# Experts' weights in a deeper ring, narrow products in full groups, and 64-place sums off TensorE

## The chip, the cores and the metric

One core of one Trainium2 chip runs the whole kernel in one launch. The metric is the device time of an execution in microseconds; the kernel before takes 1934.09 us, the median of 3 runs (1929.53 to 1937.27).

## What is computed

The reference is a two-layer backbone over 256 tokens and 256 context tokens of width 1024. Each layer mixes tokens in four branches and then channels. The change lies in the second layer's channel mixer, eight SwiGLU experts of which each token takes the best two:

```python
def _swiglu(x, wg, wu, wd):
    return (jax.nn.silu(x @ wg) * (x @ wu)) @ wd

def _moe(x, wr, br, wg, wu, wd):
    logits = (x @ wr).astype(F32)
    _, idx = lax.top_k(logits + br.astype(F32), TOP_K)
    w = jax.nn.softmax(jnp.take_along_axis(logits, idx, axis=-1), axis=-1)
    dense = jnp.sum(jax.nn.one_hot(idx, N_EXPERTS, dtype=F32) * w[..., None], axis=-2).astype(x.dtype)
    out = dense[..., 0:1] * _swiglu(x, wg[0], wu[0], wd[0])
    for e in range(1, N_EXPERTS):
        out = out + dense[..., e:e + 1] * _swiglu(x, wg[e], wu[e], wd[e])
    return out
```

x is 256 x 1024, wg and wu of an expert are 1024 x 1408, wd is 1408 x 1024, all fp32: 17.3 MB per expert.

## The kernel before

`moe` (L1210) sorts the experts on the chip by how many tokens chose them and works on the tokens that each has, gathered into places. `CAPS` gives the places by rank and `ORDER` the rank of each position, so the eight positions, e0 to e7 here, have 64, 128, 64, 128, 64, 128, 64 and 32 places; e3 (`WIDE`) has 32 more, the "thin" ones, for the rank that may overflow. The number of an expert is read from the chip's own sort at run time, so that its loads can be addressed only then.

An expert (`expert`, L1403) is 36 loads by `load_w` (L200, the DMA itself is L204): three column groups of 512, 512 and 384 columns, each with four loads of wg and four of wu (two chunks of 128 rows a load), then two halves of wd with six loads each. A load goes into a tile of the ring `raw`. All are issued by SyncE in program order, so that one load waiting for a tile holds up the ones behind it. Rings are a base, and more that `deeper` (L180) adds in a stage: raw 5 + 3 + 5 = 13 in the experts' stage, hi and lo 4 each.

For 128 places, `split_w` makes a high and a low part of each load (ScalarE copies hi, L212; VectorE subtracts lo, L213), and `mm3` (L219 to L221) multiplies in three products. With fewer places the weights are used as loaded, in fp32: `narrow` (L1388, matmul L1394) puts the chunk's places into one of the array's column groups, two groups side by side for 64 places, four for 32, so that chunk c lands in column group c modulo 2 or 4 of one PSUM tile. Each of these products shows as two records in the trace. What stands in the column groups must then be added up. `add_up` (L1397) does so: ScalarE copies the tile out of PSUM (L1399), and a matmul per 128 columns with a selection matrix (L1401) adds and turns it at once, into a PSUM tile with the hidden channels on partitions. Silu and the product of gate and up follow there, and the result `hm` goes into the down products (L1394 again, `PM<-raw,hm`). `gated` (L1478 to L1482) weighs an expert's output, and the matmul L1506 adds it into the tokens.

The order of the work on each engine is fixed when the program is built: a scheduler with priorities lays out the parts of an expert, the sums (`later`, `catch_up`) behind some products of the next group, and the gathering of the next pair's tokens (`gather_steps`, L1344) in between. PSUM has three tiles `PM`, three `PX` and one `PB`. The ring's loads are issued as far ahead as tiles come free: the first expert's begin during the layer's output projection (`out_last`, L1069). Sixteen tiles of a pool `h` are held from the first layer to the end of the program; the experts' gathered tokens (`xe`) of the 128-place experts lie in them.

Of the kernel before, what the change touches and what calls it, by code (L numbers as in the profile page):

```python
# [41 lines left out]

MORE = 5
M_TRI, M_IOTA, M_LOW, M_SEL, M_HSEL, M_ORD, M_TOP, M_CAP, M_END = 0, 128, 256, 320, 352, 416, 424, 432, 440

# [50 lines left out]
def hybrid_backbone(ctx: ExitStack, tc: tile.TileContext, A, out, dbg=None, stop=None):  # L96
# [12 lines left out]
    pool("shift", 1).tile([128, 16], F32, name="shift")  # L109
    hpool = pool("h", 16)  # L110
    spool = pool("sg", 4)
    apool = pool("ad", 2)
    col = pool("col", 4)
    pm = pool("pm", 3, space=PSUM)
    px = pool("px", 3, space=PSUM)
# [27 lines left out]
    def sg():  # L143
        return spool.tile([128, 512], F32, name="sg")
# [52 lines left out]
    def ahead_of_rest():  # L197
        return behind() if marks else tc.high_priority(offset=AHEAD)

    def load_w(src, r0, kc, c0, n, split=True, ahead=True):  # L200
        with ahead_of_rest():
            raw = wtile("raw", F32)
            r = raw[:, :kc * n].rearrange("p (k n) -> p k n", k=kc)
            nc.sync.dma_start(r, src[r0:r0 + kc * 128, c0:c0 + n].rearrange("(k p) n -> p k n", p=128))  # L204
        return split_w(raw, kc, n, ahead) if split else r
# [863 lines left out]
    def out_last(m, ax, rows, after):  # L1069

        tiles = (2, 3)
        zs = {t: [ht(F32) for _ in range(2)] for t in tiles}
        st = {t: ln_open(4) for t in tiles}
        r = load_row(S["adarows"][0, 1, 0, :], "C")
        for g in range(2):
            tok_group(A["w_out"][1], 256 * g, m, lambda t, p: add_residual(zs[t], g, p, r, ax[t], st[t]), tiles)
        w = {(g, k0): load_w(A["w_out"][1], 128 * k0, 4, 256 * g, 256) for g in (2, 3) for k0 in (0, 4)}
        for t in tiles:
            ps = pmt()
            for g in (2, 3):  # L1080
                o = ps[:, 256 * (g - 2):256 * (g - 2) + 256]
                for k in range(8):
                    wh, wl = w[g, k & 4][:2]
                    sl = slice(128 * t, 128 * t + 128)
                    mm3(o, (m[0][k][:, sl], m[1][k][:, sl]), (wh[:, k & 3, :], wl[:, k & 3, :]),
                        k == 0 and g == 2, k == 7, skip_group_check=True)
                add_residual(zs[t], g, o, r, ax[t], st[t], quick=True)
            post_ln(zs[t], st[t], rows, quick=True)
        for t in tiles:
            after(t - 2, zs[t])  # L1090
# [119 lines left out]
    def moe(R, xm):  # L1210
# [86 lines left out]

        f = [[ph(512, "f", 4) for _ in range(2)] for _ in range(2)]
        for i in range(2):
            for k in range(2):  # L1300
                with tc.issue_after(R["act"].ins):
                    nc.scalar.activation(f[i][k], xm[i][k], AF.Copy, scale=ALPHA)

        def row(src, tile_of):
# [3 lines left out]
            return r  # L1308
        sel = {THIN: mc[:, M_SEL:M_SEL + THIN], HALF: mc[:, M_HSEL:M_HSEL + HALF]}
        ad = row(S["adarows"][1, 1, 0, :], lambda: ph(512, "adr", 2))  # L1310
        ln2b = row(A["ln2_b"][1], lambda: ph(512, "l2b", 2))
        ln2g = row(A["ln2_g"][1], at)
# [31 lines left out]
        def gather_steps(out, place, weight, sizes, between=None):  # L1344
# [11 lines left out]
            def chunk(c):  # L1356
# [8 lines left out]
                if full:  # L1365
                    sh = slice(128 * full[0], 128 * full[-1] + 128)
                    sl = slice(256 + 128 * full[0], 384 + 128 * full[-1])
                    hf = sg()
                    nc.scalar.activation(hf[:, sh], ps[:, sh], AF.Identity, scale=ac[:, 4, c, 0:1], bias=ac[:, 3, c, 0:1])
                    x = ht()  # L1370
                    nc.scalar.activation(x[:, sh], hf[:, sh], AF.Copy)
                    nc.vector.tensor_tensor(x[:, sl], hf[:, sh], x[:, sh], op=OP.subtract)
                    xe.append(x)
# [22 lines left out]

        def add_up(sums, pn, n):  # L1397
            t = sg()
            nc.scalar.activation(t[:, :n], pn[:, :n], AF.Copy)  # L1399
            for i in range(n // 128):  # L1400
                nc.tensor.matmul(sums[:, i, :], t[:, 128 * i:128 * i + 128], sel[sums.shape[-1]], start=True, stop=True)  # L1401

        def expert(wge, wue, wde, q, xe, ws, dts, first=False, thin=False, last=False, small=False, side=iter(())):  # L1403

            es, el = slice(128 * q, 128 * q + 128), slice(256 + 128 * q, 384 + 128 * q)
            hT = []
# [28 lines left out]
            def gemm(src, c0, n, sums):  # L1435
                po = None if small else pmt()
                pn = (pmt() if small else pbt()) if m else None
                for k0 in range(0, 8, 2):
                    wt = load_w(src, 128 * k0, 2, c0, n, split=not small, ahead=not (first and c0 == 0))
                    for k in range(0 if small else 2):  # L1440
                        x = xe[k0 + k]
                        mm3(po[:, :n], (x[:, es], x[:, el]), (wt[0][:, k, :], wt[1][:, k, :]), k0 + k == 0, k0 + k == 7)
                    for k in range(2 if m else 0):
                        narrow(pn, k0 + k, 8, xm, (wt if small else wt[2])[:, k, :])
                    catch_up()
                if m:
                    later.append((sums, pn, n))
                go_on()
                return po
            for c0, n in ((0, 512), (512, 512), (1024, 384)):  # L1450
                j = n // 128
                both = pxt()[:, :8 * m].rearrange("p (a c m) -> p a c m", a=2, m=m) if m else None
                part = lambda a: both[:, a, :j] if m else None
                gs = sg()
# [29 lines left out]
            for hf in range(2):  # L1484
                po = pmt()
                pn = po if small else pbt() if thin else None
                for k0 in range(0, 11, 2):
                    kc = min(2, 11 - k0)
                    wt = load_w(wde, 128 * k0, kc, 512 * hf, 512, split=not small)
                    for k in range(0 if small else kc):  # L1490
                        hi, lo = hT[k0 // 4]
                        ks = slice(128 * (k0 % 4 + k), 128 * (k0 % 4 + k) + 128)
                        mm3(po, (hi[:, ks], lo[:, ks]), (wt[0][:, k, :], wt[1][:, k, :]), k0 + k == 0, k0 + k == 10)
                    for k in range(kc if m else 0):
                        narrow(pn, k0 + k, 11, hm, (wt if small else wt[2])[:, k, :])
                    catch_up()
                go_on()
# [39 lines left out]
        for e in range(NE):  # L1537
# [12 lines left out]
            if e % 2:  # L1550
                g = ahead


# [65 lines left out]
    with phase("main") as S["main"]:  # L1619
# [54 lines left out]
        pre = ctx.enter_context(phase("pre", "right"))  # L1674
        ctx.enter_context(deeper(pre, 3, 1, 1))
        S["phase"] = pre
# [16 lines left out]
    if stop == "mid1":  # L1693
        return
    with phase("moe") as S["phase"], deeper(S["phase"], 5, 0, 0):
        moe(R, xm)
# [23 lines left out]
```

## Time and profile before

| | |
|---|---|
| median of 3 runs | 1934.09 us |
| the profiled execution | 1934.3 us |
| its span | 1932.5 us |
| granted TensorE clock, mean | 0.964 |
| TensorE busy | 1811.3 us (94%) |
| VectorE, ScalarE, GpSimd busy | 1229.8, 827.1, 513.6 us |
| DMA | 337.90 MB, mean 175 GB/s |

All times below are microseconds from the span's start. The span is what the profiler's records cover; the execution's own time is 1.8 us longer. The experts' stage lies from about 1485 to 1910; after it the last sums, a normalization and the output follow. Engines: PE is TensorE's matmuls, PEld its weight loads, DVE VectorE, ACT ScalarE, POOL GpSimd, SP SyncE, with a q behind it for the DMAs it issues. A row names line, engine, operation, written and read tiles. Matmuls overlap, so several short ones hold the array for less than the sum of the times shown: a group's busy time counts the overlap once.

### The profile page before, as it was taken

What the parts mean: (1) busy time and instruction counts of PE and PEld (TensorE: products, weight loads), DVE (VectorE), ACT (ScalarE), POOL (GpSimd) and SP (SyncE); (2) the same over time, 40 slices, a digit from 0 to 9 for tenths busy, and PEclk for the clock granted to TensorE, in tenths of its full rate; (3) what the DMA queues carried; (4) which work ended last, traced back from release to release, by engine and by line L of the source; (5) the groups of instructions that cost most, each with busy time, mean ns of one, the idle gap of its engine ahead of it and who ended that gap; (6) DMA issues with size and microseconds to landing.
All of it is one profiled execution on the core that took longest, in us unless ns stands there. A gap on an engine that the chain in (4) does not pass through costs nothing. (4 is left out here: it accounts for less than half of the span.)

```text
span 1932.5 us, 29428 instructions
## 1 busy us (share of the span) xinstructions
PE 1811.3 (94%) x10954; PEld 1433.6 (74%) x10954; DVE 1229.8 (64%) x2005; ACT 827.1 (43%) x1418; POOL 513.6 (27%) x532
## 2 busy tenths in 40 slices
PE   6899989999999889999999899989997999999994
PEld 3777967788778888799789889889795584645731
DVE  5776866765555966677758955777866473534712
ACT  3444553434344553212223544755553472623610
POOL 2353625742103610022004700266231000000001
PEclk8998989999999989999999999999997999999998
DMA  8434421113313635645756542333554999569995
GB/s 307 129 91 139 120 77 55 55 61 121 99 48 121 218 109 170 197 147 190 251 186 213 161 121 61 113 99 121 175 159 154 340 372 345 183 202 393 338 366 188
DMA packets 243935, 337.90 MB, mean 175 GB/s; under 512 B 16008, under 2 KB 158864, under 8 KB 243784
## 3 DMA queue, kind: packets, MB, share of 16 engines
q1 hardware_dynamic: 235896, 318.86, 50.2%
q0 software_dynamic: 6128, 13.99, 2.3%
q10 hardware_dynamic: 1760, 3.09, 0.5%
q8 instruction: 88, 1.44, 0.3%
q14 instruction: 63, 0.52, 0.1%
HBM read 333.77 MB, written 2.12 MB: 174 GB/s over the span
## 5 line engine op out<-in xcount | busy, mean ns | idle before, releaser
L213 DVE TENSOR_TENSOR lo<-raw,hi 128x1024 fp32r<-128x1024 f32 (+1 forms) x370 | 455.1, 1240 | 168.1 <-ACT hi L212 165.4
L212 ACT ACTIVATE hi<-raw 128x1024 fp32r<-128x1024 f32 (+1 forms) x370 | 368.2, 1001 | 433.1 <-PE PM L221 166.8
L219 PE MATMUL PM<-H,hi 128*128 128x512 f32 (+1 forms) x1104 | 386.9, 353 | 7.3 <-ACT sg L1104 2.9
L220 PE MATMUL PM<-H,hi 128*128 128x512 f32 (+1 forms) x1104 | 386.0, 351 | 1.7 <-DVE H L380 1.6
L221 PE MATMUL PM<-H,lo 128*128 128x512 f32 (+1 forms) x1104 | 384.0, 351 | 0.1
L219 PEld LDWEIGHTS PM<-H,hi 128*128 128x128 f32 x1104 | 211.7, 193 | 42.3 <-issue 4.7
L220 PEld LDWEIGHTS PM<-H,hi 128*128 128x128 f32 x1104 | 211.9, 192 | 31.0 <-DVE H L380 2.4
L221 PEld LDWEIGHTS PM<-H,lo 128*128 128x128 f32 x1104 | 210.9, 192 | 29.0 <-issue 2.7
L328 DVE SCALAR_TENSOR_TENSOR ad<-raw,silu,ad 128x512 f32<-128x512 f32 x208 | 177.4, 873 | 33.7 <-issue 15.2
L219 PE MATMUL PM<-hi,H 128*128 128x256 f32 (+2 forms) x576 | 180.1, 314 | 4.3 <-ACT in L525 4.3
L220 PE MATMUL PM<-lo,H 128*128 128x256 f32 (+2 forms) x576 | 180.3, 313 | 2.4 <-DVE lo L213 2.4
L221 PE MATMUL PM<-hi,H 128*128 128x256 f32 (+2 forms) x576 | 179.2, 311 | 0.0
L1482 POOL TENSOR_TENSOR yl<-sg,yh 128x512 fp32r<-128x512 f32 x17 | 24.1, 1415 | 404.0 <-ACT yh L1481 386.7
L219 PEld LDWEIGHTS PM<-hi,H 128*128 128x128 f32 x576 | 112.6, 195 | 13.7 <-issue 5.0
L220 PEld LDWEIGHTS PM<-lo,H 128*128 128x128 f32 x576 | 112.9, 196 | 12.0 <-issue 4.1
L1020 POOL TENSOR_TENSOR B<-B,sg 128x512 f32<-128x512 f32 (+1 forms) x48 | 62.8, 1320 | 215.0 <-DVE sg L1019 198.4
L221 PEld LDWEIGHTS PM<-hi,H 128*128 128x128 f32 x576 | 112.9, 196 | 5.3 <-issue 1.4
L1394 PE MATMUL PM<-raw,xs 128*64 128x512 f32 (+3 forms) x480 | 110.7, 567 | 0.4 <-DMA raw<-in_moe_wu_dram 0.4
L805 POOL TENSOR_TENSOR C<-C,in 128x512 f32<-128x512 f32 (+1 forms) x64 | 81.3, 1295 | 76.5 <-ACT C L804 66.5
L219 PE MATMUL PM<-hi,B 128*128 128x256 f32 x352 | 98.8, 281 | 0.0
L221 PE MATMUL PM<-hi,C 128*128 128x256 f32 x352 | 98.3, 279 | 0.0
L220 PE MATMUL PM<-lo,B 128*128 128x256 f32 x352 | 98.3, 279 | 0.0
(427 smaller groups left out, 3333.3 us busy)
## 6 DMA issues: line engine op xcount, KB each, us to landing
raw<-in_w_ada_dram SPq DMA_DIRECT2D x80, 512.0 KB, 4.3
raw<-in_moe_wd_dram SPq DMA_DIRECT2D x80, 512.0 KB, 7.1
raw<-in_w_gate_dram SPq DMA_DIRECT2D x64, 512.0 KB, 3.7
raw<-in_moe_wg_dram SPq DMA_DIRECT2D x64, 512.0 KB, 5.8
raw<-in_moe_wu_dram SPq DMA_DIRECT2D x64, 512.0 KB, 7.6
raw<-in_w_in_dram SPq DMA_DIRECT2D x54, 512.0 KB, 3.6
raw<-in_ffd_wd_dram SPq DMA_DIRECT2D x28, 512.0 KB, 3.4
raw<-in_ffd_wg_dram SPq DMA_DIRECT2D x26, 512.0 KB, 3.8
```

What stands on the lines that cost most here:

```text
L212: nc.scalar.activation(h[:, :m], raw[:, :m], AF.Copy)
L213: (nc.vector if ahead else nc.gpsimd).tensor_tensor(l[:, :m], raw[:, :m], h[:, :m], op=OP.subtract)
L219: nc.tensor.matmul(o, ah, bh, start=start, stop=False, **kw)
L220: nc.tensor.matmul(o, ah, bl, start=False, stop=False, **kw)
L221: nc.tensor.matmul(o, al, bh, start=False, stop=stop, **kw)
L328: nc.vector.scalar_tensor_tensor(acc[j], part, sc, acc[j], op0=OP.mult, op1=OP.add)
L805: nc.gpsimd.tensor_tensor(E[:, xt], E[:, xt], X[:, xt], op=OP.mult)
L1020: nc.gpsimd.tensor_tensor(mixed[c][:, xt], mixed[c][:, xt], s[:, xt], op=OP.add)
L1394: nc.tensor.matmul(po[g, :w.shape[-1]], x[:, c, :], w, start=(c < k), stop=(c + k >= kk), tile_position=(0, g.start))
L1482: nc.gpsimd.tensor_tensor(yl, y, yh, op=OP.subtract)
```

## The change

Four things, all in or around the experts:

- **The ring.** `raw` has 5 + 1 + 12 = 18 tiles. Space comes from pool `h`, which is closed before the experts (`held`): `xe` gets 16 smaller tiles of its own, the two row tiles of `out_last` and the scaled residual `f` move to other tiles. For the first expert, `spare` lists the ring of each load: 6 in raw, then 8 in the tiles of hi and lo, then the 12 new tiles of raw, so that 26 loads have a tile before one is used again.
- **Full groups.** `side_by_side` collects narrow products and issues them when a set of column groups is complete: four chunks (two loads) for 32 places, two (one load) for 64.
- **64-place sums.** `add_halves` takes the place of `add_up`: ScalarE copies the upper 64 partitions out of PSUM, VectorE adds the lower 64. Silu on ScalarE and the product with up on VectorE work on 64 x 512, and a transpose per 128 columns, 11 per expert, turns the result; ScalarE copies it into `hm`.
- **A row of ln2_b** is loaded behind e6 instead of before the experts.

```diff
-        hpool = pool("h", 16)
+        held = ExitStack()
+        hpool = held.enter_context(tc.tile_pool(name="h", bufs=16))
...
-            raw = wtile("raw", F32)
+            raw = wtile(spare.pop(0) if spare else "raw", F32)
...
-        zs = {t: [ht(F32) for _ in range(2)] for t in tiles}
+        zs = {t: [ph(512, "f", 4) for _ in range(2)] for t in tiles}
...
-        f = [[ph(512, "f", 4) for _ in range(2)] for _ in range(2)]
+        f = [xm[i] for i in range(2)]
...
-                    x = ht()
-                    nc.scalar.activation(x[:, sh], hf[:, sh], AF.Copy)
+                    x = ph(256, "xe", 16, F32R)
+                    nc.scalar.activation(x[:, :128], hf[:, sh], AF.Copy)
...
+        def add_halves(pn, n):
+            t = sg()[:HALF, :n]
+            nc.scalar.activation(t, pn[HALF:, :n], AF.Copy)
+            nc.vector.tensor_tensor(t, t, pn[:HALF, :n], op=OP.add)
+            return t
+        def side_by_side(po, kk, x):
+            k = 128 // x.shape[-1]
+            got = []
+            def add(w, c):
+                got.append((c, w))
+                if len(got) == k or c == kk - 1:
+                    for c, w in got:
+                        narrow(po, c, kk, x, w)
+                    del got[:]
+                    return True
+            return add
...
-                    for k in range(2 if m else 0):
-                        narrow(pn, k0 + k, 8, xm, (wt if small else wt[2])[:, k, :])
-                    catch_up()
-                if m:
+                    if any([add((wt if small else wt[2])[:, k, :], k0 + k) for k in range(2 if m else 0)]) or not small:
+                        catch_up()
+                if m and m < HALF:
                     later.append((sums, pn, n))
...
+                if m == HALF:
+                    pg = gemm(wge, c0, n, None)
+                    h = add_halves(pg, n)
+                    nc.scalar.activation(h, h, AF.Silu)
+                    pu = gemm(wue, c0, n, None)
+                    u = add_halves(pu, n)
+                    nc.vector.tensor_tensor(h, h, u, op=OP.mult)
+                    def turned(c0=c0, j=j, h=h):
+                        pt = pxt()[:, :HALF * j].rearrange("p (c m) -> p c m", c=j)
+                        for i in range(j):
+                            nc.tensor.transpose(pt[:, i, :], h[:, 128 * i:128 * i + 128], ident[:HALF, :HALF])
+                        nc.scalar.activation(hm[:, c0 // 128:c0 // 128 + j], pt, AF.Copy)
+                    later.append(turned)
+                    continue
...
+            if e == NE - 2:
+                ln2b = row(A["ln2_b"][1], lambda: ph(8 * HALF, "xs%d" % HALF, 2))
...
-        ctx.enter_context(deeper(pre, 3, 1, 1))
+        ctx.enter_context(deeper(pre, 1, 1, 1))
...
-    with phase("moe") as S["phase"], deeper(S["phase"], 5, 0, 0):
+    held.close()
+    with phase("moe") as S["phase"], deeper(S["phase"], NRAW, 0, 0):
+        turn["raw"] = -1
+        spare.extend(["raw"] * 6 + ["hi", "lo"] * 4)
         moe(R, xm)
```

How it moves instructions, at the two places of which the prediction speaks. First TensorE in e3, from the sum of the gate's second column group into its up products, before (`xs` and `PB` are the thin places' tokens and PSUM tile, L219 to L221 the 128-place products):

```order
L1394 MATMUL PB<-raw,xs_15067 32x512 x2
L1401 MATMUL PX<-mc,sg 128x32 x4
L1394 MATMUL PB<-raw,xs_15067 32x512 x4
L220 MATMUL PM<-lo,H 128x512
L221 MATMUL PM<-hi,H 128x512
L219 MATMUL PM<-hi,H 128x512
L220 MATMUL PM<-lo,H 128x512
L221 MATMUL PM<-hi,H 128x512
L1394 MATMUL PB<-raw,xs_15067 32x512 x2
```

and with the change (L1396 is the narrow product, L1404 the selection, L1363 the gathering, L1502 a transpose, L223 to L225 the 128-place products):

```order
L1404 MATMUL PX<-mc,sg 128x32 x4
L1396 MATMUL PB<-raw,xs_15055 32x512 x8
L1363 MATMUL PX<-oh,nh 128x256
L1363 MATMUL PX<-oh,nl 128x256
L1363 MATMUL PX<-oh,nh 128x256
L1363 MATMUL PX<-oh,nl 128x256
L1502 MATMUL PX<-cst,sg 128x128 x4
```

The eight products of a column group, which came as 2, 4 and 2 with 128-place products between, stand in one run of eight. In all of e3 the narrow products stand in 21 runs of up to four (a run of eight counted as two): of the first column group's gate, four of two; then six of four at 512 columns, four of four at 384; and for the down products two of four and 4, 3, 1, 3 and 3 products.

Second TensorE in e6, from the sum of the first up product to the down products, before (`xs` and `hm` are the 64-place tokens and hidden values):

```order
L1401 MATMUL PX<-mc,sg 128x64 x4
L1394 MATMUL PM<-raw,xs_16939 64x512 x6
L1401 MATMUL PX<-mc,sg 128x64 x4
L1394 MATMUL PM<-raw,xs_16939 64x512 x4
L1394 MATMUL PM<-raw,xs_16939 64x384 x2
L1401 MATMUL PX<-mc,sg 128x64 x4
L1394 MATMUL PM<-raw,xs_16939 64x384 x8
L1401 MATMUL PX<-mc,sg 128x64 x3
L1394 MATMUL PM<-raw,xs_16939 64x384 x6
L1401 MATMUL PX<-mc,sg 128x64 x3
L1394 MATMUL PM<-raw,hm 64x512 x13
```

and with the change (L1489 is the new transpose):

```order
L1396 MATMUL PM<-raw,xs_16917 64x512 x6
L1489 MATMUL PX<-cst,sg 128x64 x4
L1396 MATMUL PM<-raw,xs_16917 64x512 x8
L1396 MATMUL PM<-raw,xs_16917 64x384 x6
L1489 MATMUL PX<-cst,sg 128x64 x4
L1396 MATMUL PM<-raw,xs_16917 64x384 x10
L1396 MATMUL PM<-raw,hm 64x512 x2
L1489 MATMUL PX<-cst,sg 128x64 x3
L1396 MATMUL PM<-raw,hm 64x512 x11
```

The sums of gate and of up, each behind some products, are gone; one run of transposes per column group is left. The last of the three stands behind two down products, where the selection before stood behind six up products of the same column group.

## Rows read from the trace of the kernel before

**Rows 1.** Windows, e0 to e7: start:end, length, engines (instructions), PEclk, DMA share, GB/s.

```profile
1485.60:1534.20 48.60, 48.60 (x217) 21.27 (x217) 9.65 (x27) 16.59 (x38) 0.00 (x0) 0.99 0.78 272
1534.20:1592.00 57.80, 57.80 (x286) 48.21 (x285) 48.60 (x57) 43.28 (x74) 3.98 (x3) 1.00 1.03 378
1592.00:1632.20 40.20, 40.20 (x194) 16.48 (x193) 7.20 (x17) 6.57 (x12) 2.55 (x2) 1.00 0.94 326
1632.20:1734.00 101.80, 101.80 (x476) 56.65 (x475) 51.87 (x61) 50.23 (x79) 4.87 (x4) 1.00 0.61 204
1734.00:1772.30 38.30, 38.30 (x184) 16.88 (x184) 6.29 (x15) 6.70 (x12) 3.79 (x3) 1.00 1.05 393
1772.30:1825.30 53.00, 52.32 (x262) 44.27 (x260) 46.67 (x49) 40.61 (x58) 3.77 (x2) 1.00 1.00 361
1825.30:1868.80 43.50, 42.09 (x205) 17.82 (x204) 7.20 (x13) 5.72 (x11) 2.55 (x2) 1.00 0.97 340
1868.80:1910.30 41.50, 34.75 (x197) 11.85 (x196) 6.52 (x12) 5.43 (x11) 2.55 (x2) 1.00 0.90 340
```

**Rows 2.** Waits, PE, 1485 to 1912: total us, times, longest.

```profile
PE PX L1401 <- ACT sg L1399: 3.6, 6, 0.7
```

**Rows 3.** Waits, SP queue, 1485 to 1912.

```profile
SPq L204 <- PE PM L1394: 95.6, 112, 5.6
SPq L204 <- PE PB L1394: 70.7, 26, 9.3
```

**Rows 4.** Groups of instructions by form, 1485 to 1912.

```profile
L1401 PE MATMUL PX<-mc,sg 128*128 128x64 f32 x176 | 23.9, 280 | 0.8 <-ACT sg L1399 0.7
...
L1399 ACT ACTIVATE sg<-PM 128x512 f32<-128x512 f32 x20 | 11.7, 596 | 40.3 <-PE PM L1394 40.3
...
L1463 PE MATMUL PX<-cst,sg 128*128 128x128 f32 x33 | 5.1, 272 | 0.0
...
L1460 DVE TENSOR_TENSOR sg<-sg,PM 128x512 f32<-128x512 f32 x6 | 4.1, 685 | 3.8 <-PE PM L221 3.4 <-ACT sg L1457 0.2
```

**Rows 5.** Timeline, PE, in e3: start, us, instruction, records.

```profile
1660.92 1.05 PE L1394 MATMUL PB<-raw,xs 128*32 128x512 f32 x4
...
1662.91 1.06 PE L1394 MATMUL PB<-raw,xs 128*32 128x512 f32 x8
1663.90 0.51 PE L220 MATMUL PM<-lo,H 128*128 128x512 f32 x1
1664.25 0.40 PE L221 MATMUL PM<-hi,H 128*128 128x512 f32 x1
1664.48 0.39 PE L219 MATMUL PM<-hi,H 128*128 128x512 f32 x1
```

**Rows 6.** Groups by form, PE, e3 (1632 to 1734).

```profile
L1394 PE MATMUL PB<-raw,xs 128*32 128x512 f32 x64 | 14.5, 604 | 0.0
...
L1394 PE MATMUL PB<-raw,hm 128*32 128x512 f32 x44 | 12.6, 605 | 0.0
...
L1394 PE MATMUL PB<-raw,xs 128*32 128x384 f32 x32 | 5.1, 498 | 0.0
```

**Rows 7.** Timeline, SP queue: start, us until the last was issued, loads.

```profile
1460.82 30.18 SPq L204 DMA_DIRECT2D raw<-in_moe_wu_dram  x5
...
1704.32 17.10 SPq L204 DMA_DIRECT2D raw<-in_moe_wu_dram  x4
```

**Rows 8.** Windows, the stage's head and end (columns as rows 1).

```profile
1460.00:1470.00 10.00, 5.88 (x39) 4.80 (x37) 9.96 (x25) 3.11 (x6) 5.30 (x9) 0.81 0.72 225
1470.00:1478.00 8.00, 3.88 (x18) 3.85 (x18) 5.55 (x20) 4.83 (x9) 1.77 (x4) 0.50 0.78 246
...
1900.00:1910.30 10.30, 8.49 (x31) 2.15 (x30) 3.65 (x6) 0.63 (x1) 1.27 (x1) 1.00 0.45 173
```

**Rows 9.** Timeline, PE, the stage's head.

```profile
1463.54 1.95 PE L1197 MATMUL PB<-wr,ad 128*128 128x8 f32 x16
...
1470.26 3.55 PE L1197 MATMUL PB<-wr,ad 128*128 128x8 f32 x16 [0.98 <-DVE pwt L226]
```

More of the change, by code (lines that the diff above doesn't have):

```diff
@@ L43 @@
 MORE = 5
+NRAW = 12
 M_TRI, M_IOTA, M_LOW, M_SEL, M_HSEL, M_ORD, M_TOP, M_CAP, M_END = 0, 128, 256, 320, 352, 416, 424, 432, 440
@@ L198, in ahead_of_rest @@
         return behind() if marks else tc.high_priority(offset=AHEAD)
+    spare = []
     def load_w(src, r0, kc, c0, n, split=True, ahead=True):
         with ahead_of_rest():
-            raw = wtile("raw", F32)
+            raw = wtile(spare.pop(0) if spare else "raw", F32)
             r = raw[:, :kc * n].rearrange("p (k n) -> p k n", k=kc)
@@ L1308, in row @@
             return r
-        sel = {THIN: mc[:, M_SEL:M_SEL + THIN], HALF: mc[:, M_HSEL:M_HSEL + HALF]}
+        sel = mc[:, M_SEL:M_SEL + THIN]
         ad = row(S["adarows"][1, 1, 0, :], lambda: ph(512, "adr", 2))
-        ln2b = row(A["ln2_b"][1], lambda: ph(512, "l2b", 2))
         ln2g = row(A["ln2_g"][1], at)
@@ L1365, in chunk @@
                 if full:
-                    sh = slice(128 * full[0], 128 * full[-1] + 128)
-                    sl = slice(256 + 128 * full[0], 384 + 128 * full[-1])
+                    sh = slice(128 * full[0], 128 * full[0] + 128)
                     hf = sg()
                     nc.scalar.activation(hf[:, sh], ps[:, sh], AF.Identity, scale=ac[:, 4, c, 0:1], bias=ac[:, 3, c, 0:1])
-                    x = ht()
-                    nc.scalar.activation(x[:, sh], hf[:, sh], AF.Copy)
-                    nc.vector.tensor_tensor(x[:, sl], hf[:, sh], x[:, sh], op=OP.subtract)
+                    x = ph(256, "xe", 16, F32R)
+                    nc.scalar.activation(x[:, :128], hf[:, sh], AF.Copy)
+                    nc.vector.tensor_tensor(x[:, 128:], hf[:, sh], x[:, :128], op=OP.subtract)
                     xe.append(x)
@@ L1400, in add_up @@
             for i in range(n // 128):
-                nc.tensor.matmul(sums[:, i, :], t[:, 128 * i:128 * i + 128], sel[sums.shape[-1]], start=True, stop=True)
+                nc.tensor.matmul(sums[:, i, :], t[:, 128 * i:128 * i + 128], sel, start=True, stop=True)
+        def add_halves(pn, n):
[14 more added lines that the diff above has]
+            return add
         def expert(wge, wue, wde, q, xe, ws, dts, first=False, thin=False, last=False, small=False, side=iter(())):
-            es, el = slice(128 * q, 128 * q + 128), slice(256 + 128 * q, 384 + 128 * q)
+            es, el = slice(0, 128), slice(128, 256)
             hT = []
@@ L1437, in gemm @@
                 pn = (pmt() if small else pbt()) if m else None
+                add = side_by_side(pn, 8, xm) if m else None
                 for k0 in range(0, 8, 2):
@@ L1442, in gemm @@
                         mm3(po[:, :n], (x[:, es], x[:, el]), (wt[0][:, k, :], wt[1][:, k, :]), k0 + k == 0, k0 + k == 7)
-                    for k in range(2 if m else 0):
-                        narrow(pn, k0 + k, 8, xm, (wt if small else wt[2])[:, k, :])
-                    catch_up()
-                if m:
+                    if any([add((wt if small else wt[2])[:, k, :], k0 + k) for k in range(2 if m else 0)]) or not small:
+                        catch_up()
+                if m and m < HALF:
                     later.append((sums, pn, n))
                 go_on()
-                return po
+                return pn if small else po
             for c0, n in ((0, 512), (512, 512), (1024, 384)):
                 j = n // 128
-                both = pxt()[:, :8 * m].rearrange("p (a c m) -> p a c m", a=2, m=m) if m else None
-                part = lambda a: both[:, a, :j] if m else None
+                both = pxt()[:, :8 * m].rearrange("p (a c m) -> p a c m", a=2, m=m) if 0 < m < HALF else None
+                part = lambda a: both[:, a, :j] if both is not None else None
+                if m == HALF:
[12 more added lines that the diff above has]
+                    continue
                 gs = sg()
@@ L1486, in expert @@
                 pn = po if small else pbt() if thin else None
+                add = side_by_side(pn, 11, hm) if m else None
                 for k0 in range(0, 11, 2):
@@ L1493, in expert @@
                         mm3(po, (hi[:, ks], lo[:, ks]), (wt[0][:, k, :], wt[1][:, k, :]), k0 + k == 0, k0 + k == 10)
-                    for k in range(kc if m else 0):
-                        narrow(pn, k0 + k, 11, hm, (wt if small else wt[2])[:, k, :])
-                    catch_up()
+                    if any([add((wt if small else wt[2])[:, k, :], k0 + k) for k in range(kc if m else 0)]) or not small:
+                        catch_up()
                 go_on()
```

2 lines of the change are left out of this document (1 added, 1 removed).

## The prediction

> **What bounds the kernel now.** I read the page first, for which stage holds what, and then only the stage that the change touches, layer 1's experts, cut by expert [rows 1]: from expert 0's first product (1485.6) to the last (1910.3) it takes 424.7 us. In e0 to e4 the PE column equals the length of the window: TensorE never idles. In e5 to e7 it falls short by 0.7, 1.4 and 6.8 us. The DMA share is full (1.0 or more) in e1, e4 and e5 and only 0.61 in e3. So TensorE sets the time as far as e5, and loads set it at the end: the reader is to see two limits, and that the second is close behind the first. The list of PE's waits for the stage agrees [rows 2]: its longest entry, copies on ScalarE, comes to 3.6 us, and loads stand below it. What the SP queue waits for [rows 3] shows why loads aren't further ahead: 95.6 and 70.7 us in which a load stood until a product gave back its tile, once for 9.3 us.
>
> What the stage moves follows from length times GB/s [rows 1]: from 1734.0 to 1910.3 it is 15.1 + 19.1 + 14.8 + 14.1 = 63.1 MB, for four experts of 17.3 MB (3 x 1024 x 1408 x 4 bytes), 69.2 MB. So 6.1 MB, some 13 loads of 0.48 MB, had been moved for e4 when e4 began: one ring of 13. The best full expert, e4, ran at 393 GB/s, 44 us for 17.3 MB.
>
> **64-place sums.** Each of e0, e2, e4 and e6 has 22 selection matmuls, 44 records of L1401 [rows 4]: 176 records, 23.9 us. They go. In their place come 11 transposes of 64 x 128 per expert, 44 in all. The nearest row is the transpose of the 128-place experts, L1463: 33 records in 5.1 us, 0.155 us each (their shown 272 ns overlap), so 44 cost 6.8 us. TensorE saves 23.9 - 6.8 = 17.1 us, 4.3 per expert. (Were a transposition as slow as the first of a run, 0.3 us, 44 would cost 13 us and the saving be 2.7 per expert; at the issue rate of 0.11 us, 4.8.)
>
> ScalarE and VectorE take over the adding. Per column group the way from the last up product to the transposes is one ScalarE copy (0.60 us) and two VectorE passes (0.69 us each) [rows 4], 2.0 us, or 1.5 us at 384 columns (by width). Before, it was the copy, 0.60, and the selection. A 64-place product comes to 0.46 us: e4's 38.3 us less 6 us of sums, over its 70 products [rows 1, 4]. Two of the three groups of an expert have at least six products of the next group ahead of the transposes, 2.8 us, so these are covered. The third, in e6, has only two ahead of it by the order shown, 0.9 us: a stall of 0.6 us and a few handovers, about 1 us, where loads are the limit. If the cover went, it is the chain rival below. VectorE and ScalarE are busy for 7 us of 40 in such an expert [rows 1], so their own time costs nothing in e2, e4 and e6; in e0 four splits of e1 stand ahead of one copy on ScalarE, each about 1 us, while e0's last products (15 of them) run.
>
> **32-place products.** They matter in e3, where 32 extra places ride on a 128-place expert and TensorE is the limit with loads to spare. Two products issued together (4 records) show 1.05 us at 1660.92, four (8 records) 1.06 us at 1662.91, with the next matmul at 1663.90, 0.99 us later [rows 5]. Two more cost nothing. The 70 products of e3 took 14.5 + 12.6 + 5.1 = 32.2 us [rows 6], in pairs for the most part; by 0.99 for each 1.06 shown that is 30.0 us from start to start. In the changed order they stand in 21 runs: 17 of 512 columns at 0.99 and 4 of 384 at 0.8 make 20.0 us. That saves 10 us, and some 11 fewer changes of product kind save 1 us (the first matmul behind one, at 1663.90, had its successor after 0.35 us, the next after 0.23 [rows 5]). Sum: **11 us**. From below the bound is 0 (if a full group costs what two pairs did), from above 16 (18 groups, none split, with the changes). A group of four waits for two loads instead of one; in e3 loads are ahead, so nobody waits. In e7 they stood in runs of four or more already wherever loads allowed.
>
> **The ring.** Up to e3 it gives TensorE nothing, since TensorE waited for no load there. The 26 loads before e0 use the time in which SP stood: its five loads from 1460.82 on took 30.2 us to be issued [rows 7]; I saw no instruction between 1460 and 1485.6 that waits for a transfer, so nothing is pushed back, and as e0 and e1 never wait for a load, nothing gained either. From e4 on it counts twice. First, e4 starts with up to 18 loads instead of 13: 5 x 0.48 = 2.4 MB that needn't be moved later. Second, fewer stalls: the 63.1 MB would take 160.6 us at 393 GB/s, but the last bytes came at about 1904.5 (1.8 MB left at 1900.0 [rows 8], 4.5 us), 170.5 us after e4's start, so 9.9 us were lost to a full ring. At the end of e3 four loads took 17.1 us to be issued [rows 7]. I keep 3 of the 9.9, for 18 tiles are shared by about five loads on the way and by pairs and fours that hold theirs until issued.
>
> The ln2_b rows move from before the experts to behind e6: 0.5 MB, 1.3 us of the DMA engines, into the stretch that they limit. On POOL's queue two issues are moved past the experts' yl work; what reads the rows comes only after the last product, and POOL is nearly idle (2.55 us of 41.5 in e7 [rows 1]). Reusing x_mid as f and the residual's tiles change no instruction's duration: nothing, as VectorE and ScalarE do the same work in the same order.
>
> **The sum.** e4 starts at 1734.0 - 4.3 (e0) - 4.3 (e2) - 11 (e3) = 1714.4. To move then: 69.2 - 6.1 - 2.4 + 0.5 = 61.2 MB, 155.7 us, to 1870.1; plus 3 of stalls, 1873.1. The last product ended 5.8 us behind the last byte (1910.3 against 1904.5); I add 1.5 for a lower clock at the end, see below: 1880.4. TensorE alone would be ready earlier: e4 34, e5 53, e6 39 us bring it to e7 at 1840.4, and e7's products need some 30 more. So loads are what is late next, and part of what the sums and the fours save is paid for in e7 as waiting. Gain: 1910.3 - 1880.4 = 29.9 us. What follows the last product is unchanged. The profiled execution took 1934.3 us, 0.2 over the median of 1934.09, so the forecast is 1934.3 - 29.9 = **1904 us**.
>
> **Rivals.**
> - *Loads stay slower.* If from e4 on they run at e5's 361 GB/s, 61.2 MB take 169.5 us, 13.8 more, less the 3 counted: 1915. For: e5 and e6 did no better. Against: SP stood waiting for tiles in them. Chance 0.12.
> - *Fours save nothing in e3* (other work fills the gap, or tiles held longer stall SP): 1915. Against: the rows at 1660.92 and 1662.91. Chance 0.07.
> - *The chain behind the 64-place products shows at every group.* Six groups of 2.0 us before e4 add 12 us: 1916; later ones hide behind loads. Against: only the third group lacks cover. The Trainium skill (TensorEngine Tiling (Array Packing), PSUM Bottleneck) warns of just this: tiling speeds up TensorE and not the copies out of PSUM, and both ScalarE and VectorE should share them. By it the chain would set the pace of these experts and the time would be this rival's; the trace shows both engines idle for over 30 of 40 us in e2, and the copies of now (L1399) held TensorE up for 3.6 us in the whole stage, so I give it little weight. Chance 0.08.
> - *More comes in than I allow:* no stall left, no clock loss, and 3 more loads ahead because e3 has DMA to spare: 3 + 1.5 + 3.7 less, 1896. Chance 0.08.
> - *Slower: TensorE's clock falls in e6 and e7.* TensorE now waits for loads there. Between 1460 and 1470 it was busy for 5.9 of 10 us; between 1470 and 1478 the granted clock was 0.50, the 1.2 GHz level, and 16 records of L1197 that took 1.95 us took 3.55 [rows 8, 9]. If e6 and e7 (39 and 35 us of work) ran so from e6's start at 1801.4, they would take 148 us: 1949, and 1973 in all. It decides once over 35 of these 74 us run at the half. Against: e7's clock stayed at 1.00 with TensorE busy 34.8 of 41.5 us, and by the sum e6 starts with loads in hand. [...] Only the last few products, 5.8 us, are a real risk, hence the 1.5 us. Chance 0.05.
>
> **How the numbers follow.** The forecast has 0.60, its own range 1898 to 1911 (sums 2.7 to 4.8 per expert, fours 9 to 16, stalls 0 to 7). The range 1894 to 1920 takes in the first four rivals' times and leaves out the slow clock and the rivals' far ends, together some 0.15. About 0.5%, 9.7 us, is what a measurement of this kernel can tell: faster is below 1924.4. Forecast 0.60, the early case 0.08, fours 0.06, chain 0.06 and slow loads 0.08 make faster 0.88; what remains of the chain and of slow loads, two of them together, makes the same 0.07; the clock makes slower 0.05.
>
> **What would show it.** L1401 only with 32 columns; transposes near 0.15 us; e0 and e2 at 44 and 36 us, e3 at 91; e4 starting near 1714; loads without a gap from there at over 385 GB/s; TensorE idle for 10 us or more in e7, for loads; last product near 1880. Wrong if e0 or e2 don't shorten, if TensorE waits over 1 us per group for VectorE, or if e4 to e7 still take 176 us.

## The result, and the profile after

The changed kernel takes 1909.22 us, the median of 4 runs (1905.72 to 1914.89), against 1935.68 us for the kernel before in the same comparison: a ratio of 0.987, with a 95% interval of 0.9834 to 0.9907. The forecast was 1904, its range 1894 to 1920. The profiled execution is the quickest of the four, 1905.72 us with a span of 1903.9; against the profile of before that is 28.6 us less span.

The page of the changed kernel, its head and TensorE's line:

```profile
span 1903.9 us, 29201 instructions
...
PE 1777.5 (93%) x10822; PEld 1411.8 (74%) x10822; DVE 1249.4 (66%) x2029; ACT 835.0 (44%) x1430; POOL 515.6 (27%) x532
```

TensorE has 33.8 us less to do than before (1811.3), which is more than the span lost. The windows of its experts, cut at each expert's last down product (columns as in [rows 1]):

```profile
1488.60:1539.10 50.50, 50.50 (x206) 21.14 (x205) 19.50 (x37) 22.50 (x44) 0.21 (x1) 0.98 0.62 216
1539.10:1599.40 60.30, 58.31 (x277) 44.75 (x277) 42.88 (x51) 40.51 (x70) 4.12 (x3) 1.00 1.04 381
1599.40:1628.70 29.30, 29.30 (x144) 11.48 (x145) 11.21 (x22) 8.97 (x16) 1.41 (x2) 1.00 0.88 321
1628.70:1712.40 83.70, 83.70 (x458) 56.06 (x459) 49.89 (x60) 46.61 (x76) 6.12 (x4) 1.00 0.74 259
1712.40:1748.80 36.40, 36.40 (x169) 13.23 (x169) 14.95 (x24) 11.91 (x19) 2.73 (x3) 1.00 1.04 377
1748.80:1805.80 57.00, 57.00 (x280) 46.94 (x280) 46.93 (x49) 38.85 (x56) 5.42 (x4) 1.00 1.05 394
1805.80:1841.80 36.00, 34.21 (x159) 11.61 (x159) 10.56 (x17) 7.50 (x14) 3.10 (x3) 1.00 0.98 348
1841.80:1881.50 39.70, 32.99 (x197) 11.78 (x196) 6.53 (x12) 5.43 (x11) 2.56 (x2) 1.00 0.89 332
```

Three things are to be seen beside [rows 1]. First, the stage is 392.9 us long and not 424.7. Here e3 is the largest part, but the order moved work across boundaries: 21 matmuls of e1 now run ahead of e0's last products, and 28 records of e2's products, not 8, ahead of e1's. So single windows should not be compared, only sums over several. Second, e0 starts at 1488.6, 3.0 us later than before. Third, TensorE idles for 2.0 us in e1, where it never did before, for 1.8 in e6 and 6.7 in e7; the granted clock is 1.00 from e1 on, so the slow rival did not come. From TensorE's list of waits, the sums of e7's 32-place products, a wait in e1 for a PSUM tile that ScalarE reads, and e7's waits for loads:

```profile
PE PX L1404 <- ACT sg L1402: 3.5, 5, 0.8
...
PE PM L223 <- ACT sg L1496: 1.5, 1, 1.5
...
PE PM L1396 <- DMA raw<-in_moe_wd_dram: 0.9, 3, 0.3
```

So half of e7's idle time belongs to the sums of its products, and little of it to loads. TensorE first idles for a load at 1866.9, in e7's down products.

The groups by form in the stage (busy us, mean ns of one, idle before them):

```profile
L1404 PE MATMUL PX<-mc,sg 128*128 128x32 f32 x88 | 11.4, 272 | 3.5 <-ACT sg L1402 3.5
...
L1410 DVE TENSOR_TENSOR sg<-sg,PM 64x512 f32<-64x512 f32 x16 | 10.8, 678 | 29.0 <-ACT sg L1409 29.0
...
L1409 ACT ACTIVATE sg<-PM 64x512 f32<-64x512 f32 x16 | 9.5, 594 | 30.3 <-PE PM L1396 30.3
...
L1484 DVE TENSOR_TENSOR sg<-sg 64x512 f32<-64x512 f32 x8 | 5.4, 680 | 0.2
L1489 PE MATMUL PX<-cst,sg 64*128 64x64 f32 x44 | 5.3, 236 | 1.1 <-DVE sg L1484 1.1
```

Only the 32-column selections are left. The 44 transposes take 5.3 us of TensorE, 0.12 each, where the selections took 23.9 [rows 4], and wait 1.1 us for VectorE in all. On half the partitions ScalarE's copy (594 ns) and VectorE's passes (678, 680) take what they took on 128 [rows 4]. e3's thin products, by form (1628 to 1715) and at one place of the timeline:

```profile
L1396 PE MATMUL PB<-raw,xs 128*32 128x512 f32 x64 | 10.0, 600 | 0.0
...
L1396 PE MATMUL PB<-raw,hm 128*32 128x512 f32 x44 | 7.2, 602 | 0.0
...
L1396 PE MATMUL PB<-raw,xs 128*32 128x384 f32 x32 | 3.0, 492 | 0.0
```

```profile
1653.63 1.92 PE L1396 MATMUL PB<-raw,xs 128*32 128x512 f32 x16
1655.48 0.39 PE L1363 MATMUL PX<-oh,nh 128*128 128x256 f32 x1
```

The three rows answer to [rows 6]: 20.2 us where 32.2 stood. Eight products leave the array after 1.85 us, 0.93 for a group of four.

What the SP queue waits for, head of the list:

```profile
SPq L208 <- PE PM L1396: 74.0, 75, 7.7
SPq L208 <- PE PB L1396: 54.4, 15, 14.3
SPq L208 <- DVE lo L217: 26.4, 32, 2.2
SPq L208 <- DMA raw<-in_moe_wg_dram: 21.6, 38, 1.4
SPq L208 <- DMA raw<-in_moe_wu_dram: 19.5, 35, 1.4
```

Loads wait for tiles 128 us instead of 166 [rows 3]. That is not the longer ring by itself: with the ring taken back (below) the two lines come to 106 us, so the list does not show what the ring is worth.

```profile
SPq L208 <- PE PB L1396: 54.8, 17, 9.5
SPq L208 <- PE PM L1396: 51.5, 75, 4.8
```

### The profile page after: what moved, and what is told of

Its sections match the earlier page's. It is cut to its first block, busy times and chain, and to the rows that moved or that the text cites. A ratio compares the mean times of both kernels' runs of the same rounds, so it can differ in the third digit from the quotient of the medians.

```text
span 1903.9 us, 29201 instructions
## 1 busy us (share of the span) xinstructions
PE 1777.5 (93%) x10822; PEld 1411.8 (74%) x10822; DVE 1249.4 (66%) x2029; ACT 835.0 (44%) x1430; POOL 515.6 (27%) x532
## 3 DMA queue, kind: packets, MB, share of 16 engines
q1 hardware_dynamic: 235896, 318.86, 50.5%
## 5 line engine op out<-in xcount | busy, mean ns | idle before, releaser
L223 PE MATMUL PM<-H,hi 128*128 128x512 f32 (+1 forms) x1104 | 388.0, 354 | 7.5 <-ACT sg L1108 2.9
L225 PE MATMUL PM<-H,lo 128*128 128x512 f32 (+1 forms) x1104 | 384.9, 351 | 0.0
L223 PEld LDWEIGHTS PM<-H,hi 128*128 128x128 f32 x1104 | 211.3, 192 | 44.3 <-issue 4.4
L224 PEld LDWEIGHTS PM<-H,hi 128*128 128x128 f32 x1104 | 211.5, 192 | 32.2 <-issue 2.0
L225 PEld LDWEIGHTS PM<-H,lo 128*128 128x128 f32 x1104 | 210.5, 191 | 31.8 <-issue 2.7
L223 PE MATMUL PM<-hi,H 128*128 128x256 f32 x432 | 127.2, 295 | 4.1 <-ACT in L529 4.1
L224 PE MATMUL PM<-lo,H 128*128 128x256 f32 x432 | 126.7, 293 | 1.9 <-DVE lo L217 1.9
L225 PE MATMUL PM<-hi,H 128*128 128x256 f32 x432 | 126.1, 292 | 0.0
L1396 PE MATMUL PM<-raw,xs 128*64 128x512 f32 (+3 forms) x448 | 99.9, 565 | 0.0
L223 PE MATMUL PM<-hi,B 128*128 128x256 f32 x352 | 98.6, 280 | 0.0
L225 PE MATMUL PM<-hi,C 128*128 128x256 f32 x352 | 98.1, 279 | 0.0
L223 PEld LDWEIGHTS PM<-hi,H 128*128 128x128 f32 x432 | 86.3, 200 | 5.7 <-ACT in L529 4.3
L224 PEld LDWEIGHTS PM<-lo,H 128*128 128x128 f32 x432 | 86.4, 200 | 4.1 <-DVE lo L217 2.2
L225 PEld LDWEIGHTS PM<-hi,H 128*128 128x128 f32 x432 | 86.4, 200 | 0.8 <-issue 0.8
```

The costliest lines, as they stand in the source:

```text
L223: nc.tensor.matmul(o, ah, bh, start=start, stop=False, **kw)
L224: nc.tensor.matmul(o, ah, bl, start=False, stop=False, **kw)
L225: nc.tensor.matmul(o, al, bh, start=False, stop=stop, **kw)
L1396: nc.tensor.matmul(po[g, :w.shape[-1]], x[:, c, :], w, start=(c < k), stop=(c + k >= kk), tile_position=(0, g.start))
```

## The experiments

For each kernel the trace of one execution gives where the experts begin, the time from there to the end of e3's last 128-place down product, from there to the end of e7's last down product (the stage is the sum), and the runs give a median:

| kernel | e0 begins | e0 to e3 | e4 to e7 | stage | median |
|---|---|---|---|---|---|
| before | 1485.6 | 246.1 | 175.4 | 421.5 | 1935 to 1937 |
| before again | 1484.6 | 246.3 | 176.1 | 422.4 | one run, 1934.2 |
| changed | 1488.7 | 223.7 | 166.0 | 389.7 | 1909.2 |
| sums taken back | 1495.4 | 235.6 | 171.3 | 406.9 | 1926.4 |
| fours taken back | 1488.9 | 232.9 | 167.3 | 400.3 | 1921.0 |
| ring taken back | 1493.3 | 227.5 | 173.3 | 400.9 | 1921.3 |
| ring alone | 1494.5 | 248.6 | 165.1 | 413.5 | 1932.5 |
| sums alone | 1490.6 | 241.3 | 171.4 | 412.8 | 1932.7 |
| fours alone | 1497.2 | 233.4 | 178.9 | 412.2 | 1933.2 |
| no extra tiles for e0 | 1491.5 | 226.4 | 165.8 | 392.3 | 1911.7 |
| four loads more, e6 | 1492.8 | 222.7 | 169.7 | 392.4 | 1910.5 |
| four loads more, e3 | 1490.6 | 229.9 | 166.7 | 396.5 | 1919.3 |
| longer chain | 1492.4 | 229.0 | 166.8 | 395.7 | 1916.2 |
| other order | 1494.9 | | | 401.6 | 1921.8 |

The cut at e3's end is one by place, not by work: some of e4's products stand ahead of it (18 records before, 12 changed, 26 with the sums taken back, 32 with the ring alone), and some thin products of e3 behind it. Where this matters, the text below gives the two parts counted by expert, with those products put where they belong; by that count the change gains 20.2 us in e0 to e3 and 11.7 in e4 to e7.

**Sums taken back.**

```diff
-                if m and m < HALF:
+                if m:
                     later.append((sums, pn, n))
...
-                if m == HALF:
+                if False:
```

> The changed kernel with the 64-place sums as before (selection matmuls on TensorE). Theory (TensorE is the limit up to e3, loads from e4 on): e0 and e2 get 4.3 us longer each and shift everything; what e4 and e6 lose hides behind loads. So 8.6 us more than the changed kernel, about 1914 us in a profiled execution against 1905.7, and the idle time of TensorE in e7 shrinks. Rival, TensorE the limit throughout: 17 us more, 1923. Rival, the chain of copies behind the 64-place products is exposed: no more, or less time than the changed kernel.

Measured: a ratio to before of 0.994 (0.9921 to 0.9958), 1926.4 us, 17 us more than the changed kernel. The stage is 17.2 us longer, as the rival had it. Counted by expert, 9.9 of these lie in e0 to e3, where 8.6 were expected, and 7.3 in e4 to e7, where none was: in that kernel loads do not hide the sums of e4 and e6.

**Fours taken back.**

```diff
-            k = 128 // x.shape[-1]
+            k = 2
             got = []
```

> The changed kernel with 32-place products issued in pairs, as each load comes. Theory: e3 gets 11 to 16 us longer (11 by my sum, 16 if every pair stands alone), all of it before the loads become the limit, so 11 to 16 us more than the changed kernel: 1917 to 1922. Rival, fours save nothing in e3 because other work or held tiles eat it: within 3 us of the changed kernel.

Measured: 0.9918 (0.9899 to 0.9936), 1921.0 us, 11.8 more than the changed kernel, in the stage 10.6. From start to start e3's thin products take 27.3 us instead of 19.1. As expected.

**Ring taken back.**

```diff
-NRAW = 12
+NRAW = 7
...
-        spare.extend(["raw"] * 6 + ["hi", "lo"] * 4)
```

> The changed kernel with 13 raw tiles in the experts' stage (5 + 1 + 7), and no tiles of hi and lo for the first expert. Theory: e4 starts as early as with 18, but with 2.4 MB less in hand (6 us) and with the stalls of the ring back (up to 7 us): 6 to 13 us more than the changed kernel, 1912 to 1919. Rival, the ring is worth nothing since only TensorE counts: within 3 us. Rival, the ring is what made the gain: 20 us or more.

Measured: 0.9925 (0.9908 to 0.9943), 1921.3 us, 12.1 more; in the stage 11.2, 7.3 of it in e4 to e7, where the ring was expected to act. The rest, 3.8 us, is about made up by two things: thin products stand in 23 runs instead of 21 (counted as in the prediction, a run of eight as two) and take 21.6 us, not 19.1, and TensorE idles for 3.5 us in e1 and e2 instead of 2.0. The number of tiles changes the order that the scheduler builds.

**Ring alone.** Both product edits above taken back at once.

> The changed kernel with both product changes taken back: 18 raw tiles and 26 loads for the first expert alone. Theory: e4 starts where it did before (246 us behind e0's start), the loads from there are done 6 to 13 us earlier: 1921 to 1928 us, so 15 to 22 more than the changed kernel. Rival, TensorE the limit throughout: no gain on the kernel before, 1934.

Measured: 0.9979 (0.9966 to 0.9992), 1932.5 us. The median says that the ring alone gains 3 us, and both theories miss. The stage is 8.0 us shorter; counted by expert, e4 to e7 are 7.0 us shorter, near the lower end of the 6 to 13 that were expected, and e0 to e3 1.0. But in the profiled execution this kernel's experts begin 9 us later than before's, and that takes it back. This execution is 3 us above the median, so part of the 9 us is spread (see "Before again").

**Sums alone and fours alone.** The edits of "fours taken back" and "ring taken back" together, and those of "sums" and "ring".

> The changed kernel with pairs instead of fours and 13 raw tiles without the first expert's extra tiles: the 64-place sums are the only large part left. If TensorE is the limit up to e6 (what the undone sums point to), four experts get 4.3 us shorter and e7 gives back some of it as waiting for loads: 10 to 17 us less than the kernel before, 1919 to 1926 by the medians. If loads limited from e4 on, as in the prediction, only e0 and e2 count: 9 us less, 1927.

> The changed kernel with the sums on TensorE and 13 raw tiles without the first expert's extra tiles: the fours are the only large part left. e3's thin products should take 19 to 22 us from start to start instead of 30, so 8 to 11 us less than the kernel before, less what the shorter ring takes back when a four holds two loads: 1925 to 1930 by the medians. If a ring of 13 eats them, within 3 us of the kernel before.

Measured: 0.9982 (0.9969 to 0.9994) and 0.9989 (0.9976 to 1.0002), 2 us each where at least 9 and at least 4 were expected. Again the stage shows the gain, 8.7 and 9.3 us, and the experts begin 5 and 12 us later. In the stage of sums alone, e0 to e3 gain 4.8 us and not 8.6. Of the difference 3.5 us are idle time of TensorE that was not there before: 1.8 for the transposes, which wait for VectorE, 1.1 for a split and 0.6 for ScalarE. The two longest entries of its list of waits, over the whole stage:

```profile
PE PX L1545 <- ACT yh L1520: 3.7, 5, 1.1
PE PX L1489 <- DVE sg L1484: 3.6, 4, 0.9
```

In fours alone, counted by expert, e0 to e3 gain 10.6 us and e4 to e7 give 1.2 back. That loads which a ring of 13 had not let in are the reason is not shown.

By the stage, where what comes ahead of it does not enter, the parts are thus worth 8.0, 8.7 and 9.3 us alone, 26.0 in sum, and 31.8 together. Of the 5.8 us between them 2.5 are measured: with the fours alone the thin products stand in 23 runs, in the changed kernel in 21. The rest was not taken apart.

**Before again.** The kernel before, unchanged.

> The kernel before once more, for its trace. In the profiles of all the kernels with the change the experts begin 3 to 10 us later than in the one profile of before (1485.6). If that is the spread of executions, this profile begins later too, by some us; if the change delays what comes ahead of the experts, it begins within 2 us of 1485.6.

Measured: it begins at 1484.6. All twelve profiles of kernels with the change (that of the changed kernel and eleven variants) begin between 1488.7 and 1497.2, 7.5 us later on average than the two of before. So the change delays what comes ahead of the experts. One part of the delay is a change of order. VectorE between 1374 and 1382, before:

```profile
1374.49 1.29 DVE L946 TENSOR_REDUCE mx<-PX 128x1 f32<-128x512 f32 x2 [0.59 <-PE PX L944]
1376.13 1.38 DVE L946 TENSOR_REDUCE mx<-PX 128x1 f32<-128x512 f32 x2 [0.35 <-PE PX L944]
1378.42 0.23 DVE L1173 TENSOR_TENSOR wrp<-wr,adac 128x64 f32<-128x64 f32 x1 [0.91 <-DMA wr<-in_moe_wr_dram]
```

and with the change:

```profile
1376.71 1.29 DVE L950 TENSOR_REDUCE mx<-PX 128x1 f32<-128x512 f32 x2 [0.59 <-PE PX L948]
1381.52 0.23 DVE L1177 TENSOR_TENSOR wrp<-wr,adac 128x64 f32<-128x64 f32 x1 [3.52 <-DMA wr<-in_moe_wr_dram]
1381.78 0.22 DVE L1178 TENSOR_TENSOR wr<-wr,adac 128x64 f32<-128x64 f32 x1
1381.93 0.68 DVE L950 TENSOR_REDUCE mx<-PX 128x1 f32<-128x512 f32 x1
```

The router's weights are multiplied (wrp) once their load has landed. Before, four row maxima of the attention stood ahead of that; now two of them stand behind it and wait with it, 3.5 us instead of 0.9, and TensorE behind them. The shift of this kernel against before grows there from 2.2 to 4.4 us. The reverse comes some 100 us later and gives back 0.9 us in each of the twelve. Since f is now scaled in place, ScalarE has two of these copies, not four, ahead of the normalization step for which VectorE and then TensorE wait; before, and with the change:

```profile
1470.91 2.18 ACT L1302 ACTIVATE f<-H 128x512 f32<-128x512 f32 x4
...
1474.88 1.14 ACT L1306 ACTIVATE f<-f 128x512 f32<-128x512 f32 x2
```

The rest, some 5 us on average over the twelve, gathers in small pieces over the first 1350 us, where instructions and their order are the same. Most of it is not spread. Between 936 and 991, where TensorE never idles and the granted clock is 1.00, each of the twelve loses 0.99 us and before again nothing: the same products take a few ns more each. Two groups of that stretch, before and with the change:

```profile
L219 PE MATMUL PM<-H,hi 128*128 128x512 f32 x78 | 30.7, 394 | 0.0
L220 PE MATMUL PM<-H,hi 128*128 128x512 f32 x78 | 30.4, 390 | 0.0
...
L223 PE MATMUL PM<-H,hi 128*128 128x512 f32 x78 | 31.0, 398 | 0.0
L224 PE MATMUL PM<-H,hi 128*128 128x512 f32 x78 | 30.9, 396 | 0.0
```

Four stretches at that clock (421 to 644, 725 to 830, 936 to 1035, 1177 to 1209) cost the changed kernel 4.9 us in all, and before again 0.0. What the change moves there is where tiles lie, since pool h is opened behind others; that this is the cause was not tried, and neither was a version with the router's product back in its place. The differences among the twelve, on the other hand, go for the most part with the granted clock of the one execution that was profiled: a mean of 0.966 with the fours taken back (experts from 1488.9), 0.959 with the ring alone (1494.5). Executions of the ring alone run from 1925.6 us at 0.969 to 1937.9 at 0.960.

**No extra tiles for e0.**

```diff
-        spare.extend(["raw"] * 6 + ["hi", "lo"] * 4)
```

> The changed kernel with 18 raw tiles, but without the eight loads into tiles of hi and lo for the first expert. Theory: TensorE waited for no load in e0 to e3, so nothing: within 3 us of the changed kernel in the stage. Rival: the 26 loads are what carries e0 to e2, up to 10 us more.

Measured: 0.9881 (0.9864 to 0.9899) against 0.987: no difference that can be told. The stage is 2.6 us longer, and the thin products of e3 account for it (23 runs, 21.6 us, against 21 and 19.1). No worth of the 26 loads ahead can be seen.

**Four loads more, ahead of e6 and ahead of e3.** Nobody reads them.

```diff
                 W = (flat(wg, n), flat(wu, n), flat(wd, n))
+            if e == 6:
+                for k0 in range(0, 8, 2):
+                    load_w(W[0], 128 * k0, 2, 0, 512, split=False)
```

> The changed kernel with four more loads of 512 KB, which nobody reads, ahead of e6's own. If loads are the limit from e4 to the end (the prediction's sum), the end moves by their transfer time, 4 x 1.32 us = 5.3 us. If TensorE is the limit up to e6 and there are loads in hand, e6 hides part of it: 0 to 3 us. The undone sums cost 17 us and not 8.6, which speaks for TensorE.

> The same four loads ahead of e3's own, where the DMA share was 0.61 before. Both theories: within 2 us of the changed kernel. If it costs 5 us too, transfers are the limit everywhere and the ring decides everything.

Measured: 0.9858 (0.9844 to 0.9872) with the loads in e6, no slower than the changed kernel; its stage is 2.7 us longer, half of the transfer time. In its windows the DMA engines take up what they had left over:

```profile
1805.80:1842.00 36.20, 33.27 (x158) 11.75 (x159) 10.50 (x17) 7.48 (x14) 3.10 (x3) 1.00 1.05 390
1842.00:1888.00 46.00, 37.95 (x206) 12.44 (x202) 6.38 (x12) 5.43 (x11) 2.55 (x2) 1.00 0.87 325
```

The first of them has a share of 1.05 where the changed kernel had 0.98. So transfers were not the whole limit of e6. In e3, where the loads should have cost nothing, the kernel took 1919.3 us (0.9909, 0.9895 to 0.9923), 10 more, and 6.8 in the stage. 2.5 of them are runs again, 23 instead of 21: four tiles out of turn shift the ring and the order with it. The rest of the 6.8 stays open, and the run says nothing about transfers.

**Longer chain.**

```diff
             nc.scalar.activation(t, pn[HALF:, :n], AF.Copy)
+            nc.scalar.activation(t, t, AF.Copy)
             nc.vector.tensor_tensor(t, t, pn[:HALF, :n], op=OP.add)
+            nc.vector.tensor_copy(t, t)
             return t
```

> The changed kernel with the work behind every 64-place product lengthened: one more ScalarE copy and one more VectorE copy in place, 1.3 us more from the last up product to the transposes. If two of three groups are covered, as predicted, only the third group of each expert shows it: 0 to 5 us in all. If the chain is exposed at every group: 12 x 1.3 = 15 us more.

Measured: 0.9894 (0.988 to 0.9908), 1916.2 us; the stage is 6.0 us longer, with 4.1 more in e0 (54.5 instead of 50.4), 1.8 in e2 and 0.7 each in e4 and e6. That is 1 us above what "covered" allowed, and far from 15. What appears is a wait that the prediction did not name, from its list of PE's waits:

```profile
PE PM L1396 <- DVE sg L1411: 2.2, 1, 2.2
PE PX L1491 <- DVE sg L1486: 1.8, 2, 1.0
```

The first is a product waiting for a PSUM tile that add_halves has not read yet; the transposes' wait, the one that was predicted, is the second.

**Other order.**

```diff
-ORDER = (0, 2, 4, 1, 5, 3, 6, 7)
+ORDER = (0, 4, 1, 5, 2, 6, 3, 7)
```

> The changed kernel with the experts in another order of ranks: places 64, 64, 128 + 32, 64, 128, 64, 128, 32. Theory: at the end e5 and e6 of now are 64-place experts' neighbours with 44 us of transfers each, and TensorE idles 6 us in e7 and 2 in e6; behind a 128-place expert the ring is full when the last, 32-place one starts, so up to 8 us of waiting go: 1898 to 1906 against 1905.7. Rival, the waits in e7 aren't for loads in hand but for its own short chains: no change. Rival, slower: two 64-place experts at the start run out of loads (2 x 35 us of TensorE against 2 x 44 us of transfers, with 26 loads ahead), up to 10 us more.

Measured: 0.9919 (0.9903 to 0.9935), 1921.8 us, 12.6 more, 11.9 in the stage. The waits in e7 did shrink (4.6 us in all instead of 6.4, and none for a load any more), but the list of PE's waits is headed by the same PSUM tiles:

```profile
PE PM L1396 <- DVE sg L1410: 8.6, 6, 2.0
```

The two longest, 2.0 and 1.9 us, fall in e1, a 64-place expert that now follows another. The other four, 4.7 us, fall in e3 and e5, which stand between 128-place experts as in the changed kernel, where no such wait is longer than 0.15 us. So the chain rival is real in another order of the work, but that neighbours decide it is not shown. Another 2.7 us are thin products (21.8 us from start to start, not 19.1). No version tried here beats the changed kernel.

## Why the prediction was right

- **64-place sums: 4.3 us per expert.** The price of the operations was right to a little: 5.3 us for the 44 transposes instead of 6.8. The cover was too: 1.1 us of waiting for VectorE in the whole stage, for about 1 that was predicted. With the ring taken back the wait is 3.6 us, and sums alone gained 4.8 us in e0 to e3 rather than 8.6. A cost that the prediction did not name is e1's wait of 1.5 us for a PSUM tile.
- **32-place products: 11 us.** 19.1 us from start to start where 20.0 were predicted and 30.1 stood; taken back, 10.6 us in the stage. A four costs no more than a pair did, 0.93 us against 0.98.
- **The ring: 6 us of loads in hand and 7 of stalls, less 1.3 for ln2_b.** Oversized. Counted by expert, e4 to e7 gain 7.0 us with it alone and lose 7.4 when it is taken back, for 11.7; the 11.2 of the whole stage holds the other order of e3 and the waits in e1 and e2. The loads in hand were right, the stalls were not (next point). Nothing for the first expert's 26 loads, as said.
- **The sum.** The stage lost 31.8 us, 29.9 were forecast. Cut as in the prediction, e4 to e7 take 166.6 us (1714.75 to 1881.3), for 166.0 in the sum. Two small misses cancel in this, which is luck:

```profile
1714.75:1881.30 166.55, 158.24 (x784) 82.44 (x783) 76.45 (x97) 63.06 (x99) 13.31 (x11) 1.00 1.00 366
...
1875.00:1877.40 2.40, 2.10 (x13) 0.36 (x10) 0.97 (x2) 0.00 (x0) 0.00 (x0) 1.00 0.17 64
```

  61.0 MB are moved, for 61.2 in the sum, but the last of it comes at about 1875.4, 160.7 us after the start: some 5.6 us of stalls, where 3 were allowed. The last product ends 5.9 us later, as before, and the 1.5 us for a lower clock were not needed. That e4 starts at the forecast's 1714 is luck too: e0 starts 3.0 us late, and by this cut e0 to e3 gained 2.7 more than the 19.6 forecast.
- **"So loads are what is late next" from e4 on** was half right. By it, undone sums should cost only e0's and e2's share, 8.6 us, and four more loads 5.3; they cost 17.2 and 2.7. TensorE sets the pace through e6, and loads hold it only in e7's down products, from 1866.9 on. The two limits lie so close that the sum by one alone gave nearly the right time. Of the 10 us or more that TensorE was to idle in e7 for loads, 6.7 came, 0.9 of them in its listed waits for loads.
- **"VectorE and ScalarE do the same work in the same order"**, so nothing from the moved tiles, failed. Ahead of the experts VectorE's order changed at the router's product and ScalarE's at the scaling of f, and the same products came a few ns later each; the kernels with the change come to e0 7.5 us later on average (3.0 in the profile). This is why the profiled execution gained 28.6 us and not the stage's 31.8. That the median, 1909.2, lies another 3.5 us above the profiled execution is spread (1905.7 to 1914.9).
- **The signs.** "Wrong if e0 or e2 don't shorten": e0's window grew from 48.6 to 50.5 us. That is e1's work moved into it, for with the ring taken back, where none is, e0 takes 44.8. The loads did not keep over 385 GB/s from e4 on: 61.0 MB in 160.7 us are 379.
- **The rivals.** Fours that save nothing, loads that stay at 361 GB/s (e5 ran at 394) and the clock in e6 (1.00) are refuted by the profile. The chain did not show at every group here. The Trainium skill's warning that copies out of PSUM may become the bottleneck (TensorEngine Tiling (Array Packing), PSUM Bottleneck) agrees with the trace of the other order, where TensorE waits 8.6 us for PSUM tiles.

## What to carry to other kernels

Three edits to one stage gained 2 to 3 us each in the median and 26 together, since each kernel with one of them alone pays the same loss ahead of the stage. Take each part's worth from the stage's own length and from the whole with that part taken back, not from the part alone. Look at what a change in pools does far ahead of the edit: one step moved past a late load held VectorE for 3.5 us, and unchanged products took some ns more each. Where work moves across a boundary, count it by whose it is, not by where the cut falls. And where narrow products run side by side in the array, issue full sets: the third and fourth cost no more time here.

## What the runs showed of the hardware that was not expected

- ScalarE's copy and VectorE's passes take the same time on 64 partitions as on 128: 594 against 596 ns, 678 against 685.
- Four 32-place fp32 products of 512 columns leave the array 0.93 us after they began, as two do (0.98, with the fours taken back); a run of eight takes 1.85.
- The same products in the same order, at a granted clock of 1.00 and without idle time, took 390 and 394 ns before and 396 and 398 with the change, alike in all twelve kernels with it; the repeat of before has the numbers of before. Only where tiles lie differs there, and that this is the cause was not tried.
